# Gated DeltaNet stage: the triangular inverse without breaks beside z and v, masks first on GpSimd, convolutions in halves of their rows, the two chains at their own ticks

## The chip, the cores and the metric

The kernel runs on one core of one Trainium2 chip. The metric is the device time of one execution in microseconds (us); with several runs, their median. The engines are called by the profile's names: PE (TensorE, the matrix engine), DVE (VectorE), ACT (ScalarE), POOL (GpSimd) and SP (SyncE, which here issues the loads of the weights). SBUF is the memory on the chip, PSUM the small one that PE writes.

## The reference

Two decoder layers over 256 tokens of width 1024, in float32. Each layer is half a SwiGLU feed-forward (hidden width 2816), a token mixer, and half a feed-forward again, each behind an RMSNorm and added to the stream. Layer 1's mixer is sliding-window attention, which the change leaves alone. Layer 0's is a gated DeltaNet:

```python
proj = h @ w_in                                   # q, k, v, z: 1024 columns each; b, a: 8
qkv = silu(causal_depthwise_conv(qkv, w_conv))    # 4 taps along the tokens
q = l2norm(q) * 128 ** -0.5; k = l2norm(k)        # 8 heads of 128
beta = sigmoid(b); g = -exp(A_log) * softplus(a + dt_bias)
...
L = where(strict, (k * beta) @ k.T * decay, 0)
u, w = (I + L)^-1 [v * beta, k * beta * exp(g)]   # triangular solve per chunk and head
v_new = u - w @ S;  o = (q * exp(g)) @ S + a_qk @ v_new;  S = S * gl + k_dec.T @ v_new
...
o = rmsnorm(o, out_norm) * silu(z);  x += o @ w_out
```

What is computed is thus: projections, short convolutions, a triangular inverse per head, a recurrence over chunks of tokens, a gated norm and an output projection.

## The kernel before, in words

The kernel is one program for one core, written with a tile framework. Its scheduler fixes ahead of time in which order each engine runs its instructions; generators ("tickers") tell it in which order the pieces are offered, and `issue_after` keeps an instruction behind another. The framework's tile pools hand out a fixed number of buffers, and the first write to a tile waits until the readers of the buffer's last owner are done. Two pools matter here: psA and psB, four PSUM buffers each. Weights pass through four raw buffers and five pairs of split buffers.

A float32 product is made of three PE passes (`mm3`): each operand is split into a rounded high and a low part. Weights are split on the chip: SP loads 512 KB (`split`, L288), ACT casts the high part (L310), and DVE (L312, one instruction of 1024 columns) or POOL (L317, four of 256) takes the difference. A "chunk" is 256 columns of `w_in`, made of two such pieces (rows 0 to 511 and 512 to 1023).

The DeltaNet stage `gdn` works through chunks: z0, z1, z2, then k0 to k3, v0 to v3, q0 to q2, z3, q3. For a chunk of q, k or v, `conv` (L918) projects two tiles of 128 channels x 256 tokens, one after the other, 24 matmuls of 256 columns each into a psA buffer; ACT takes the last tap (L925), DVE the other three (L928, one instruction each, read from PSUM), and ACT's silu writes the result (L932). After each tile the ticker moves every active generator by one step.

- `gdn_gates` (L602): decay and beta from b and a, tiny DVE steps (L626 to L649), then the cumulative sums `pcum` on PE and the decay matrices `Dt`.
- `kpost` (L725): transposes k on PE (`pkn`), copies it on ACT (L729, L730), sums squares on ACT (`sumsq`, L717: four squares with an accumulator, L721), forms k k^T (`pkk`), and per chunk the factors `br` and `nbr` and two scalings of `kk2` on POOL (L747, L748).
- `blocks` (L756), for each half of the heads: cuts diagonal blocks, masks them on POOL (L768, L770) and takes a power for the norm (L772).
- `inverse` (L775): inverts the 16x16 diagonal blocks of all heads on DVE alone (L780 to L818), 24 steps, with a `yield` at two places, between which the taps of convolutions are offered.
- `chain` (L822), for each half of the heads: widens the inverse to 32, 64 and 128 with small PE matmuls (L833 `pt1`, `py`; L853; L865; L873; L881; L887), each step followed by one on ACT or DVE. Both chains are added to the ticker at the inverse's end and step together.
- `state` (L1014), `u_of` (`puu`), `pwt`, `pS`, `pws`: the recurrence over the two chunks of tokens; `o_of` (`po`, L1039), `post` (L1048: ACT square L1051, DVE sum L1052, L1054, POOL power L1055, DVE scaling L1057) and `turn` (L1062: transposes `poT`, ACT cast L1068, DVE difference L1069) end in the output projection (`acc`, `out_part`, L526).

Of the kernel before, what the change touches and what calls it, by code (L numbers as in the profile page):

```python
# [213 lines left out]
class Kern:  # L214
    def __init__(self, ctx, tc):
# [11 lines left out]
        self.early = None  # L227

# [59 lines left out]
    def split(self, src, hi, lo, shape, eng=None, cuts=1):  # L288
# [9 lines left out]
        with ExitStack() as behind:  # L298
# [14 lines left out]
            if eng is not None:  # L313

                r, h, l = (a.rearrange("p a b -> p (a b)").rearrange("p (n f) -> p n f", f=256) for a in (raw, hi, lo))
                for i in range(4):
                    eng.tensor_tensor(out=l[:, i], in0=r[:, i], in1=h[:, i].bitcast(F32), op=ALU.subtract)  # L317
# [10 lines left out]
    def wcols(self, w, c0, npool=0):  # L328
        src = w[:, c0:c0 + 256].rearrange("(k p) f -> p k f", p=P)
        pieces = [self.wpiece(src[:, 4 * i:4 * i + 4, :], 4, 256,  # L330
                              eng=self.nc.gpsimd if i >= 2 - npool else None) for i in range(2)]
        return lambda k, cs: tuple(a[:, k % 4, cs] for a in pieces[k // 4])
# [47 lines left out]
    def proj_T(self, out, w, f, nrm):  # L380
        fs = slice(f * P, (f + 1) * P)
        for k in range(KT):
            wh, wl = w(k, fs)
            self.mm3(out, wh, wl, nrm.h.hi(k), nrm.h.lo(k), k == 0, k == KT - 1)
# [296 lines left out]
    def gdn(self, nrm, prep, w_in, w_out, after):  # L681
# [9 lines left out]
        tk = Ticker()  # L691
        Dt = self.big([P, NT, H, P], "Dt")
# [32 lines left out]
        def kpost(c):  # L725
# [3 lines left out]
            nc.scalar.copy(kd[:, hs, :], pv[:, 0])  # L729
            nc.scalar.copy(keg[:, hs, :], pv[:, 1])  # L730
            sumsq(pv, ssk, 2 * c)
            yield
            beta, eG, eS = res["beta"], res["eG"], res["eS"]
# [7 lines left out]
            a = ssk[:, :, hs]  # L741
            nc.vector.tensor_scalar_add(a, a, EPS)
            nc.vector.reciprocal(br[:, :, hs], a)
            nc.vector.tensor_mul(br[:, :, hs], br[:, :, hs], beta[:, :, hs])
            nc.vector.tensor_scalar_mul(nbr[:, :, hs], br[:, :, hs], -1.0)
            yield
            nc.gpsimd.tensor_tensor(out=kd[:, hs, :], in0=kd[:, hs, :], in1=bc(eS, 0, hs), op=ALU.mult)  # L747
            nc.gpsimd.tensor_tensor(out=keg[:, hs, :], in0=keg[:, hs, :], in1=bc(eG, 1, hs), op=ALU.mult)  # L748
# [7 lines left out]
        def blocks(g):  # L756
# [4 lines left out]
            us = slice(8 * g, 8 * g + 8)  # L761
            raw = self.y1([P, 8, 32], "d32")
# [6 lines left out]
            for j, m in enumerate(("tri16", "off16")):  # L769
                nc.gpsimd.tensor_tensor(out=d2[:, j, us, :], in0=raw,  # L770
                                        in1=M[m].unsqueeze(1).to_broadcast([P, 8, 32]), op=ALU.mult)
            nc.gpsimd.tensor_tensor(out=sv[:, :, gs], in0=ssk[:, :, gs],  # L772
                                    in1=self.phalf.rearrange("p (t h) -> p t h", t=NT), op=ALU.pow)

        def inverse():  # L775
# [21 lines left out]
            yield  # L797
# [13 lines left out]
            yield  # L811
# [6 lines left out]
            nc.vector.transpose(yx[:, 1].rearrange("p u c -> p (u c)"), yx[:, 0].rearrange("p u c -> p (u c)"))  # L818
            late["yx"] = yx
            tk.add(chain(0), chain(1))  # L820

        def chain(g):  # L822
# [6 lines left out]
            def blockwise(ps, lhsT, rhs):  # L829
                for i in range(8):  # L830
                    for b in range(4):
                        bs = slice(32 * b, 32 * b + 32)
                        nc.tensor.matmul(ps[bs, i * 32:i * 32 + 32], lhsT=lhsT[bs, i, :], rhs=rhs[bs, i, :],  # L833
                                         start=True, stop=True)
# [15 lines left out]
            for i in range(8):  # L850
                for b in (0, 2):
                    e, o = slice(32 * b, 32 * b + 32), slice(32 * b + 32, 32 * b + 64)
                    nc.tensor.matmul(pt[o, i * 32:i * 32 + 32], lhsT=nf[e, i, o], rhs=X[e, i, :], start=True, stop=True)  # L853
# [8 lines left out]
            for i in range(8):  # L862
                for b in (0, 2):
                    e, o = slice(32 * b, 32 * b + 32), slice(32 * b + 32, 32 * b + 64)
                    nc.tensor.matmul(py[e, i * 32:i * 32 + 32], lhsT=t32[o, i, :], rhs=Y[o, i, :], start=True, stop=True)  # L865
# [52 lines left out]
        def conv(col0, dst, npool, start):  # L918
            w = self.wcols(w_in, col0, npool)
            for f in range(2):  # L920
                ct = col0 // P + f
                ps = self.psA("pcv")
                self.proj_T(ps[:, :T], w, f, nrm)
                c = self.c1([P, T], "cv")
                nc.scalar.activation(c, ps[:, :T], AF.Copy, scale=wc[:, 3, ct:ct + 1])  # L925
# [5 lines left out]
                with self.tc.issue_after(res["exp"].ins):  # L931
                    nc.scalar.activation(dst(f), c, AF.Silu)  # L932
                tk.tick()
            tk.add(*start, first=True)

        def zproj(c, t, w):
            pz = self.psA("pz")
            self.proj_N(pz[:, :T], w, t, nrm)
            hs = slice(2 * c, 2 * c + 2)
            nc.scalar.copy(zs[:, t, hs, :], pz[:, :T].rearrange("p (h c) -> p h c", h=2))  # L940

        def zgate(t, hs, keep=lambda ins: ins):
            z = zs[:, t, hs]
            keep(nc.scalar.activation(z, z, AF.Silu))
            keep(nc.gpsimd.tensor_tensor(
                out=z, in0=z, in1=onb.unsqueeze(1).to_broadcast([P, hs.stop - hs.start, P]), op=ALU.mult))
# [7 lines left out]
        def then(*steps):  # L954
            for st in steps:
                r = st()
                if r is not None:
                    yield from r
                    yield
# [11 lines left out]
        def zmore(n):  # L971
            for c in range(zc[0], zc[0] + n):
                w = self.wcols(w_in, 3 * D + c * 256)
                for t in range(NT):
                    zproj(c, t, w)
# [399 lines left out]
```

## Time and profile before

| what | value |
| --- | --- |
| median of 3 runs (lowest, highest) | 1019.48 us (1018.77, 1020.96) |
| the profiled execution | 1017.73 us |
| its span in the trace | 1016.0 us |
| mean granted PE clock | 0.996 |
| DeltaNet stage | from 200 to 376 us of the span, about |

The trace tells each instruction's start and length. A row of the waits names the waiting line and the one that released it, then the total, the number and the longest. The windows give each engine's busy time in a stretch, and behind them the granted PE clock, as a share of full speed. A row of groups ends with the count, the busy time, the mean of one in ns, and the idle time of the engine just ahead of them. A row of the timeline starts with the start and the length; matmuls overlap, so their pace is read from the starts.

### The profile page before, as it was taken

To read this page: it belongs to the slowest core of one execution; us is meant where nothing else is said; L and a number is where in the kernel's file an instruction comes from. 1 tells how busy PE (TensorE), PEld (TensorE's weight loads), DVE (VectorE), ACT (ScalarE), POOL (GpSimd) and SP (SyncE) were. 2 spreads that over 40 slices of the span, in tenths; PEclk is the share of its full clock that TensorE was granted. 3 is DMA by queue.
4 is the path that set the end of the run, shared out by engine and by line. 5 is a ranking of instruction groups with operands and counts; after the bars stand their busy time and mean duration, and the time that the engine had idled before them with its cause. 6 is when DMAs were issued, how large, how long until landed. Compare 5 with 4: busy or idle time off the path is not lost.

```text
span 1016.0 us, 16483 instructions
## 1 busy us (share of the span) xinstructions
PE 998.0 (98%) x6195; PEld 870.7 (86%) x6195; DVE 643.7 (63%) x975; ACT 547.8 (54%) x979; POOL 242.1 (24%) x311
## 2 busy tenths in 40 slices
PE   8999999999989999999999999999999999999997
PEld 7888888899979888888888888888898678888886
DVE  5866654666895766666546666664578756666544
ACT  5756544457856445555434655553467545555442
POOL 0125510017952301323100123320021402222100
PEclk9999999999999999999999999999999999999999
DMA  7766666644452337666666666665563426666661
GB/s 246 235 188 191 200 197 182 205 129 148 133 175 65 105 104 208 195 188 197 191 199 190 186 187 186 192 207 189 185 209 104 152 91 212 190 189 187 203 188 43
DMA packets 135316, 177.05 MB, mean 174 GB/s; under 512 B 7250, under 2 KB 120260, under 8 KB 135236
## 3 DMA queue, kind: packets, MB, share of 16 engines
q1 hardware_dynamic: 132032, 171.46, 55.3%
q10 hardware_dynamic: 3204, 4.53, 1.4%
q8 instruction: 49, 0.80, 0.3%
q14 instruction: 31, 0.25, 0.1%
HBM read 174.92 MB, written 1.05 MB: 173 GB/s over the span
## 4 chain that ended last, share of the span: by engine, by line
PE 89%; DVE 4%; ACT 3%; issue 1%; DMA 1%; POOL 1%; SPq 1%; POOLq 0%; ACTq 0%
PE pg L370 14%; PE pu L370 14%; PE acc L365 9%; PE acc L363 9%; PE acc L364 9%; PE pu L371 7%; PE pg L371 7%; PE pgu L365 2%; PE pgu L364 2%; PE pgu L363 2%; DVE wlo L312 1%; DMA raw<-in_ffn_w_gu_dram 1%; PE pcv L363 1%; PE pcv L364 1%; PE pcv L365 1%
## 5 line engine op out<-in xcount | busy, mean ns | idle before, releaser
L312 DVE TENSOR_TENSOR wlo<-raw,whi 128x1024 fp32r<-128x1024 f32 (+1 forms) x304 | 374.9, 1236 | 198.0 <-ACT whi L310 196.8
L310 ACT CAST whi<-raw 128x1024 fp32r<-128x1024 f32 (+1 forms) x318 | 330.3, 1046 | 179.5 <-PE acc L365 83.2
L370 PE MATMUL pg<-hs,whi 128*128 128x512 f32 x624 | 218.7, 392 | 0.0
L370 PE MATMUL pu<-hs,whi 128*128 128x512 f32 x624 | 218.4, 392 | 0.0
L371 PE MATMUL pu<-hs,wlo 128*128 128x256 f32 x624 | 175.4, 281 | 0.0
L371 PE MATMUL pg<-hs,wlo 128*128 128x256 f32 x624 | 174.6, 281 | 0.0
L478 POOL TENSOR_TENSOR act<-act,gate 128x256 f32<-128x256 f32 x78 | 58.6, 751 | 352.0 <-DVE act L477 337.4
L370 PEld LDWEIGHTS pg<-hs,whi 128*128 128x128 f32 x624 | 116.9, 187 | 25.3
L370 PEld LDWEIGHTS pu<-hs,whi 128*128 128x128 f32 x624 | 116.9, 187 | 25.2
L364 PE MATMUL acc<-wlo,ah 128*128 128x512 f32 (+1 forms) x340 | 128.6, 378 | 0.0
L365 PE MATMUL acc<-whi,al 128*128 128x512 f32 (+1 forms) x340 | 128.5, 378 | 0.0
L363 PE MATMUL acc<-whi,ah 128*128 128x512 f32 (+1 forms) x340 | 128.0, 378 | 0.0
L371 PEld LDWEIGHTS pg<-hs,wlo 128*128 128x128 f32 x624 | 118.2, 189 | 0.4
L371 PEld LDWEIGHTS pu<-hs,wlo 128*128 128x128 f32 x624 | 118.2, 189 | 0.0
L363 PEld LDWEIGHTS acc<-whi,ah 128*128 128x128 f32 x340 | 64.0, 188 | 12.0
L364 PEld LDWEIGHTS acc<-wlo,ah 128*128 128x128 f32 x340 | 64.0, 188 | 11.8
L365 PEld LDWEIGHTS acc<-whi,al 128*128 128x128 f32 x340 | 64.0, 188 | 11.9
L481 POOL TENSOR_SCALAR ah<-act 128x256 fp32r<-128x256 f32 x78 | 66.4, 852 | 6.7
L467 ACT COPY gate<-pg 128x256 f32<-128x256 f32 x78 | 28.7, 368 | 55.6 <-PE pg L371 55.6
L476 ACT COPY act<-pu 128x256 f32<-128x256 f32 x78 | 28.7, 368 | 54.1 <-PE pu L371 54.1
L363 PE MATMUL pcv<-hs,whi 128*128 128x256 f32 x192 | 55.1, 287 | 2.2 <-DVE cv L928 2.2
L99 POOL TENSOR_TENSOR rst<-var,mhalf 128x1 f32<-128x1 f32 x10 | 5.6, 557 | 215.6 <-DVE var L97 215.6
(340 smaller groups left out, 1576.6 us busy)
## 6 DMA issues: line engine op xcount, KB each, us to landing
raw<-in_ffn_w_gu_dram SPq DMA_DIRECT2D x156, 512.0 KB, 4.4
raw<-in_ffn_w_down_dram SPq DMA_DIRECT2D x88, 512.0 KB, 4.2
raw<-in_a_w_in_dram SPq DMA_DIRECT2D x32, 512.0 KB, 4.2
raw<-in_ffn_w_gu_dram SPq DMA_DIRECT2D x40, 256.0 KB, 4.7
raw<-in_b_w_in_dram SPq DMA_DIRECT2D x12, 512.0 KB, 4.8
raw<-in_a_w_out_dram SPq DMA_DIRECT2D x8, 512.0 KB, 3.7
raw<-in_b_w_out_dram SPq DMA_DIRECT2D x8, 512.0 KB, 3.7
nw<-in_ffn_norm_dram ACTq DMA_DIRECT2D x3, 512.0 KB, 4.0
```

Of the source, the lines that this page charges most:

```text
L99: nc.gpsimd.tensor_tensor(out=r, in0=v, in1=k.mhalf[:, 0:1], op=ALU.pow)
L310: nc.scalar.copy(hi[:, c], raw[:, c])
L312: nc.vector.tensor_tensor(out=lo[:, c], in0=raw[:, c], in1=hi[:, c].bitcast(F32), op=ALU.subtract)
L363: nc.tensor.matmul(out, lhsT=lh, rhs=rh, start=start, stop=False)
L364: nc.tensor.matmul(out, lhsT=lh, rhs=rl, start=False, stop=False)
L365: return nc.tensor.matmul(out, lhsT=ll, rhs=rh, start=False, stop=stop)
L370: nc.tensor.matmul(out, lhsT=lh, rhs=r2, start=start, stop=False)
L371: return nc.tensor.matmul(out[:, :T], lhsT=ll, rhs=rh, start=False, stop=stop)
L467: nc.scalar.copy(g, pg[:, T:])
L476: nc.scalar.copy(a, pu[:, T:])
L478: nc.gpsimd.tensor_tensor(out=a, in0=a, in1=gates[f], op=ALU.mult)
L481: ahead[2] = nc.gpsimd.tensor_scalar(oh, a, 1.0, None, op0=ALU.mult)
```

## The change

- `sumsq` squares the four transposes in place in PSUM with one ACT instruction and sums with one DVE reduce. `kpost` copies both halves of `kk2` with one ACT copy. `br` and `nbr` are made once for each half of the heads, in `blocks`, and the eight scalings of `kk2` on POOL move to `kscale`, behind v2's POOL splits.
- The power leaves `blocks`: `roots` puts the first half's behind that half's masks, the second's behind v1's splits. With `self.masks`, v1's POOL splits are put behind the second half's masks.
- `inverse` has no `yield` any more. The chains are not added at its end but after v2, each to a ticker of its own (`tkc`), and `conv` ticks the one behind each half of its first tile, the other behind its second's. The chains' matmuls are put behind the projection's last offered matmul (`late["mm"]`).
- `conv` takes both psA tiles at once and runs rows 0 to 511 of both tiles, then rows 512 to 1023 of both. The taps are a function of their own; v1's are put behind the end of the inverse.
- z3 moves from behind q2 to behind v0, in halves too, with its second piece split on POOL. POOL's share of the splits changes: the second piece of k1 and k2 (before: of k2 and k3), nothing of v0, both pieces of v1 (before: the second of each v chunk); v2 and v3 keep theirs. The gate of z on POOL is cut into pieces of 256 columns.

The diff, cut to its core:

```diff
         def sumsq(pv, ss, h0):
-            for i in range(2):
-                for t in range(NT):
-                    j = self.small([P, P], "junk", 1)
-                    nc.scalar.activation(j, pv[:, t, i, :], AF.Square, accum_out=ss[:, t, h0 + i:h0 + i + 1])
+            nc.scalar.activation(pv, pv, AF.Square)
+            nc.vector.tensor_reduce(out=ss[:, :, h0:h0 + 2], in_=pv, axis=AX.X, op=ALU.add)
...
+        def kscale():
+            eG, eS = res["eG"], res["eS"]
+            for c in range(4):
+                hs = slice(2 * c, 2 * c + 2)
+                with self.tc.issue_after(late["short"].ins):
+                    nc.gpsimd.tensor_tensor(out=kd[:, hs, :], in0=kd[:, hs, :], in1=bc(eS, 0, hs), op=ALU.mult)
+                    nc.gpsimd.tensor_tensor(out=keg[:, hs, :], in0=keg[:, hs, :], in1=bc(eG, 1, hs), op=ALU.mult)
+                yield
...
+        def roots(g, behind):
+            gs = slice(4 * g, 4 * g + 4)
+            with self.tc.issue_after(behind.ins):
+                nc.gpsimd.tensor_tensor(out=sv[:, :, gs], in0=ssk[:, :, gs],
+                                        in1=self.phalf.rearrange("p (t h) -> p t h", t=NT), op=ALU.pow)
...
                 nc.vector.tensor_add(y, y, tmp)
-            yield
             for h in (4, 8):
...
-            yield
             nc.vector.tensor_copy(t1.rearrange("p c (h r) -> p c h r", h=2),
...
-            tk.add(chain(0), chain(1))
...
             def blockwise(ps, lhsT, rhs):
-                for i in range(8):
...
+                with self.tc.issue_after(late["mm"].ins):
+                    for i in range(8):
...
-        def conv(col0, dst, npool, start):
+        def conv(col0, dst, npool, start, behind=None):
             w = self.wcols(w_in, col0, npool)
-            for f in range(2):
-                ct = col0 // P + f
-                ps = self.psA("pcv")
-                self.proj_T(ps[:, :T], w, f, nrm)
...
+            acc = [self.psA("pcv") for f in range(2)]
+            for half in range(2):
+                for f in range(2):
+                    late["mm"] = self.proj_T(acc[f][:, :T], w, f, nrm, range(4 * half, 4 * half + 4))
+                    tkc[f].tick()
+                    if half:
+                        taps(col0 // P + f, acc[f], dst(f), behind)
+                        tk.tick()
+            tk.add(*start, first=True)
+
+        def taps(ct, ps, dst, behind):
+            c = self.c1([P, T], "cv")
+            nc.scalar.activation(c, ps[:, :T], AF.Copy, scale=wc[:, 3, ct:ct + 1])
+            with ExitStack() as later:
+                if behind is not None:
+                    later.enter_context(self.tc.issue_after(behind.ins))
...
-            conv(D + c * 256, lambda f: kT[:, 2 * c + f, :], c // 2, [then(*steps)])
+            conv(D + c * 256, lambda f: kT[:, 2 * c + f, :], int(c in (1, 2)), [then(*steps)])
...
-            conv(2 * D + c * 256, lambda f: vT[:, f, :], 1, [vpost(c, vT)])
+            self.masks = late["d"] if c == 1 else None
+            conv(2 * D + c * 256, lambda f: vT[:, f, :], ((), (0, 1), (1,), (1,))[c], [vpost(c, vT)],
+                 late["inv"] if c == 1 else None)
+            if c == 0:
+                zmore(1)
+            if c == 1:
+                roots(1, self.short)
+            if c == 2:
+                late["short"] = self.short
+                for g in range(2):
+                    tkc[g].add(chain(g))
+                tk.add(kscale())
...
-            if c == 2:
-                n = 2 * zc[0]
-                w = self.wcols(w_in, 3 * D + 3 * 256)
-                for t in range(NT):
-                    zproj(3, t, w)
-                    zgate(t, slice(n, H))
-                    tk.tick()
-        tk.drain()
+        for ticker in (*tkc, tk):
+            ticker.drain()
```

The scheduler turns this into new orders. First, DVE at the end of the inverse, before. The inverse's tiles are `inv`, `tw` and `yx`; `cv` are the taps, here of q's chunks (`pcv_3323`, `pcv_3393` and `pcv_3467` are PSUM tiles of q0's second, q1's first and q1's second tile), `wlo` the splits of weights.

```order
L810 TENSOR_REDUCE inv_2793<-tw_2790 128x8x8
L928 SCALAR_TENSOR_TENSOR cv_3348<-pcv_3323,wc_1902,cv_3348 128x255
L928 SCALAR_TENSOR_TENSOR cv_3418<-pcv_3393,wc_1902,cv_3418 128x255
L812 COPY tw_2790<-inv_2793 128x512
L928 SCALAR_TENSOR_TENSOR cv_3348<-pcv_3323,wc_1902,cv_3348 128x254
L928 SCALAR_TENSOR_TENSOR cv_3418<-pcv_3393,wc_1902,cv_3418 128x254
L815 STREAM_TRANSPOSE tw_2790<-tw_2790 128x16x32
L928 SCALAR_TENSOR_TENSOR cv_3348<-pcv_3323,wc_1902,cv_3348 128x253
L312 TENSOR_TENSOR wlo_3675<-raw_3676,whi_3674 128x1024
L928 SCALAR_TENSOR_TENSOR cv_3418<-pcv_3393,wc_1902,cv_3418 128x253
L816 TENSOR_TENSOR yx_2906<-tw_2790,blk16_953 128x512
L312 TENSOR_TENSOR wlo_3795<-raw_3796,whi_3794 128x1024
```

And the same place now; `pcv_2814` and `pcv_2815` are v1's two tiles, `pcv_2893` and `pcv_2894` v2's.

```order
L313 TENSOR_TENSOR wlo_3206<-raw_3207,whi_3205 128x1024
L832 STREAM_TRANSPOSE yx_2697<-yx_2697 128x512
L957 SCALAR_TENSOR_TENSOR cv_2852<-pcv_2814,wc_1902,cv_2852 128x255
L957 SCALAR_TENSOR_TENSOR cv_2870<-pcv_2815,wc_1902,cv_2870 128x255
L957 SCALAR_TENSOR_TENSOR cv_2931<-pcv_2893,wc_1902,cv_2931 128x255
L957 SCALAR_TENSOR_TENSOR cv_2958<-pcv_2894,wc_1902,cv_2958 128x255
L957 SCALAR_TENSOR_TENSOR cv_2852<-pcv_2814,wc_1902,cv_2852 128x254
L957 SCALAR_TENSOR_TENSOR cv_2870<-pcv_2815,wc_1902,cv_2870 128x254
L957 SCALAR_TENSOR_TENSOR cv_2931<-pcv_2893,wc_1902,cv_2931 128x254
L957 SCALAR_TENSOR_TENSOR cv_2958<-pcv_2894,wc_1902,cv_2958 128x254
L313 TENSOR_TENSOR wlo_3391<-raw_3392,whi_3390 128x1024
L957 SCALAR_TENSOR_TENSOR cv_2852<-pcv_2814,wc_1902,cv_2852 128x253
```

Before, taps of q stand between the inverse's steps. Now DVE runs 25 rows, of which 23 are the inverse's, from its first step to its last, with only two splits of weights inside, then eight taps of v1 and v2, a split and the third tap of v1's first tile. The next matmul on PE behind v2 is v3's first, into `pcv_2980`, the fifth psA tile counted from `pcv_2814`.

Second, PE at the end of the stage, before: `po` are the outputs of heads (`po_3942`, `po_3958` and, one turn later, `po_4004`), `acc` the output projection, `poT` the transposes of normalized outputs.

```order
L1004 MATMUL po_3958<-u_2634,Dt_1904 128x128
L364 MATMUL acc_3979<-wlo_3899,oT_3228 128x512
L365 MATMUL acc_3979<-whi_3898,oT_3228 128x512
L363 MATMUL acc_3979<-whi_3904,oT_3228 128x512
L364 MATMUL acc_3979<-wlo_3905,oT_3228 128x512
L365 MATMUL acc_3979<-whi_3904,oT_3228 128x512
L363 MATMUL acc_3979<-whi_3910,oT_3228 128x512
L364 MATMUL acc_3979<-wlo_3911,oT_3228 128x512
L365 MATMUL acc_3979<-whi_3910,oT_3228 128x512
L1004 MATMUL po_4004<-S_3227,wq_1907 128x128
L1004 MATMUL po_4004<-u_2634,Dt_1904 128x128
L1004 MATMUL po_4004<-S_3227,wq_1907 128x128
```

Five more of `po_4004` follow there, and then `poT_4024`. Now (`po_3887`, `po_3903`, then `po_3949`, and `poT_3969`):

```order
L1049 MATMUL po_3903<-u_2592,Dt_1904 128x128
L1049 MATMUL po_3887<-u_2592,Dt_1904 128x128 x2
L1049 MATMUL po_3949<-S_3202,wq_1907 128x128
L1049 MATMUL po_3949<-u_2592,Dt_1904 128x128
L1049 MATMUL po_3949<-S_3202,wq_1907 128x128
L1049 MATMUL po_3949<-u_2592,Dt_1904 128x128
L1049 MATMUL po_3949<-S_3202,wq_1907 128x128
L1049 MATMUL po_3949<-u_2592,Dt_1904 128x128
L1049 MATMUL po_3949<-S_3202,wq_1907 128x128
L1049 MATMUL po_3949<-u_2592,Dt_1904 128x128
L1110 MATMUL poT_3969<-ident_70,on_3893 128x128 x4
L368 MATMUL acc_3923<-whi2_3864,oT_3203 128x512
```

The eight matmuls of the output projection between the two turns of `po` are gone from that place; they stand ahead of `po` now.

More of the change, by code (lines that the diff above doesn't have):

```diff
@@ L315, in split @@
                 r, h, l = (a.rearrange("p a b -> p (a b)").rearrange("p (n f) -> p n f", f=256) for a in (raw, hi, lo))
-                for i in range(4):
-                    eng.tensor_tensor(out=l[:, i], in0=r[:, i], in1=h[:, i].bitcast(F32), op=ALU.subtract)
+                with ExitStack() as masks:
+                    if self.masks is not None:
+                        masks.enter_context(self.tc.issue_after(self.masks.ins))
+                    for i in range(4):
+                        self.short = eng.tensor_tensor(out=l[:, i], in0=r[:, i], in1=h[:, i].bitcast(F32), op=ALU.subtract)
     def wpiece(self, src, a, b, eng=None, pool=None):
@@ L691, in gdn @@
         tk = Ticker()
+        tkc = [Ticker() for g in range(2)]
         Dt = self.big([P, NT, H, P], "Dt")
@@ L930, in conv @@
                         in1=c[:, s:], op0=ALU.mult, op1=ALU.add)
[L931 to L934 removed]
+            with self.tc.issue_after(res["exp"].ins):
+                nc.scalar.activation(dst, c, AF.Silu)
         def zproj(c, t, w):
```

79 lines of the change are left out of this document (43 added, 36 removed).

## The prediction

> **What bounds the kernel now.** First I read the page for the engine that sets the time.
>
> ```profile
> PE 998.0 (98%) x6195; PEld 870.7 (86%) x6195; DVE 643.7 (63%) x975; ACT 547.8 (54%) x979; POOL 242.1 (24%) x311
> ```
>
> TensorE (PE) is busy for 98% of the span. No matmul is removed or added, so the change can only win or lose time in which PE stands still or runs at a lower clock. The waits of PE in the DeltaNet stage (200 to 376 us, the only stage whose code changes), and the windows in which they fall, are next.
>
> ```profile
> PE pcv L363 <- DVE cv L928: 2.2, 2, 1.5
> PE py L833 <- ACT t L837: 2.0, 1, 2.0
> PE acc L363 <- ACT oT L1068: 0.7, 1, 0.7
> PE pt L833 <- DVE yx L818: 0.5, 1, 0.5
> PE pt L853 <- DVE X L844: 0.5, 1, 0.5
> ```
>
> ```profile
> 280.00:290.00 10.00, 8.50 (x71) 8.33 (x71) 10.00 (x21) 5.95 (x10) 4.60 (x5) 1.00 0.62 182
> 290.00:300.00 10.00, 8.34 (x184) 7.68 (x183) 10.00 (x14) 4.61 (x8) 7.43 (x8) 1.00 0.42 141
> 300.00:310.00 10.00, 8.03 (x224) 7.69 (x225) 8.23 (x20) 6.33 (x18) 2.35 (x3) 0.83 0.34 111
> ```
>
> The columns behind the window's length are PE, weight loads, DVE, ACT, POOL (busy us and count), then the granted clock. From 280 to 300 DVE is busy without a gap and PE waits for it; from 300 to 310 the clock is 0.83, which costs 1.7 us more. The rows of waits add up to 5.9 us. A wait costs somewhat more than its row says:
>
> ```profile
> 283.05 0.28 PE L364 MATMUL pcv<-hs,whi 128*128 128x256 f32 x1
> 283.17 0.28 PE L365 MATMUL pcv<-hs,wlo 128*128 128x256 f32 x1
> 284.95 0.36 PE L363 MATMUL pcv<-hs,whi 128*128 128x256 f32 x1 [1.50 <-DVE cv L928]
> ```
>
> A matmul of 256 columns starts 0.12 us after the one before it; here 1.78 us pass, so the wait of 1.50 costs 1.66. With 0.16 for each of six waits, **before loses 5.9 + 1.0 + 1.7 = 8.6 us** in this stage. That is all that the change can win.
>
> **The convolutions' first part (k).** The gates' pcum stands after 67 projection matmuls of k in PE's order now, after 99 before: 32 x 0.12 = 3.8 us earlier. It needs gg from DVE.
>
> ```profile
> 222.60 0.17 DVE L642 TENSOR_SCALAR gr<-gr 128x16 f32<-128x16 f32 x1
> 222.81 0.63 DVE L641 TENSOR_TENSOR gr<-gr,gs 128x16 f32<-128x16 f32 x1
> 227.58 0.17 DVE L647 SCALAR_TENSOR_TENSOR gg<-gr,expA 128x16 f32<-128x16 f32 x1
> 222.68 2.83 POOL L317 TENSOR_TENSOR wlo<-raw,whi 128x256 fp32r<-128x256 f32 x4 [23.38 <-ACT whi L310]
> 228.99 0.29 PE L652 MATMUL pcum<-gg,sufftri 128*128 128x16 f32 x2
> ```
>
> gg ends at 227.75, 1.24 us before PE's use, so 3.8 - 1.2 = 2.6 us would be missing. DVE is rid of one split of 1.22 us ahead of it, since POOL takes k's second chunk now: 1.4 at row prices, and I take 1.0 (0 to 2.2), as four of the tiny operations ran into POOL's split (0.63 instead of 0.17) and may not do so where the order differs. The squares of k leave ACT's four pairs for one pass and a DVE reduce. That shortens ACT, but the PSUM tile of the transposes is now given back by DVE, in order behind its taps. Nearest below is nothing, above the 1.5 us of the longest wait for a tap; I take 0.8, of which the waits of two later transposes are made. POOL's half of v1, v2 and z can come late (POOL does 12 such splits in a row): 0.4 to 1.2, I take 0.8.
>
> **The inverse in one go.** This is the term that decides. All of its steps, eight taps and three weight splits now follow each other on DVE (the order under the change shows them), and v3's first matmul waits for the ninth tap, because psA has four buffers: v3's first tile takes the one of v1's first half, whose three taps are put behind the inverse. So between the end of v0 and v3 PE has z's 48 matmuls, 96 of v1 and v2 and four transposes, and no more.
>
> ```profile
> 298.87 0.66 PE L714 MATMUL pvn<-ident,vT 128*128 128x128 f32 x4
> 270.00:298.00 28.00, 8.80 (x17) 1.00 0.55 172
> 270.00:298.00 28.00, 1.75 (x4) 1.00 0.55 172
> L784 DVE COPY inv<-inv 128x256 f32<-128x256 f32 x1 | 0.8, 826 | 0.0
> L818 DVE STREAM_TRANSPOSE yx<-yx 128x512 f32<-128x512 f32 x1 | 0.7, 695 | 0.0
> 280.21 1.22 DVE L312 TENSOR_TENSOR wlo<-raw,whi 128x1024 fp32r<-128x1024 f32 x1
> 297.50 1.60 DVE L928 SCALAR_TENSOR_TENSOR cv<-pcv,wc,cv 128x255 f32<-128x255 f32 x4
> L925 ACT ACTIVATE cv<-pcv,wc 128x256 f32<-128x256 f32 x24 | 11.2, 472 | 4.3 <-PE pcv L365 4.3
> ```
>
> The two rows of 28 us are DVE's busy time with the inverse's tiles tw and itmp. PE's cover is 144 x 0.12 + 4 x 0.13 = 17.8 us, and 0.8 more with POOL's late pieces: 18.6. DVE's chain from the end of v0: ACT's copy 0.5, three taps of 0.40, a tiny step 0.3, a split 1.2, together 3.2; the inverse 8.8 + 1.75 + 0.83 + 0.70 = 12.1; two splits inside it 2.4; eight taps 3.2; another split 1.2; the ninth tap 0.4. Sum 22.5, so **PE would wait 3.9 us** even if nothing is late. Two things make it later. The mask from POOL hangs on the last sum of squares, on four tiny steps and on two POOL operations:
>
> ```profile
> L768 POOL TENSOR_TENSOR d<-d,knbr 128x256 f32<-128x256 f32 x2 | 1.2, 618 | 0.0
> L770 POOL TENSOR_TENSOR d<-d,tri 128x256 f32<-128x256 f32 x2 | 1.5, 740 | 0.1
> ```
>
> Copy, square and reduce of 0.6 to 0.7 each from 1.4 us ahead of v0's end, tiny steps of 0.65, 0.62 and 0.74 end about 3.9 us after it, 0.7 behind DVE's own 3.2. And POOL works beside the whole inverse: 8 splits of v1, a power, 4 of v2, 8 scalings, 4 of v3, some 19 us. A neighbour of that kind shows in the trace:
>
> ```profile
> 273.04 1.75 DVE L312 TENSOR_TENSOR wlo<-raw,whi 128x1024 fp32r<-128x1024 f32 x1
> 272.09 6.84 POOL L317 TENSOR_TENSOR wlo<-raw,whi 128x256 fp32r<-128x256 f32 x8
> ```
>
> DVE's split took 1.75 instead of 1.22 while POOL split. About half of the inverse already ran beside POOL in before, so I add 0.5 for each of three splits and for two steps that did not: 2.5 (0 to 5). The wait ahead of v3 is then 3.9 + 0.7 + 2.5 = 7.1 us (2 to 11). The Trainium skill, page "SBUF — State Buffer", section "Who interferes with whom", says that a DVE instruction with two SBUF inputs and a GpSimd instruction lock each other out for a whole instruction. The tiny steps above (0.17 alone, 0.63 beside POOL) agree; by the rule alone each such step of the inverse would wait out a POOL operation of 0.7, which is the third rival.
>
> After the 2.0 us wait for t the clock fell to half for 3.4 us (the 0.83 of that window), so I put the same 1.7 us (0 to 3.4) behind the longer wait.
>
> **The chains later.** Spread over q, each chain step has conv matmuls between it and the next, which hide ACT's and DVE's 1 to 2 us. The waits for yx, t and X go; I count nothing in their place. But state(), u for the second half and po come later too, behind the last q conv, with less work around them. In before they had this:
>
> ```profile
> 344.69 1.27 ACT L1051 ACTIVATE on<-po 128x512 f32<-128x512 f32 x2 [2.97 <-PE po L1004]
> 345.32 1.36 DVE L1052 TENSOR_REDUCE so<-on 128x4 f32<-128x512 f32 x2 [1.67 <-ACT on L1051]
> 346.59 0.28 DVE L1054 TENSOR_TENSOR fo<-ssq,so 128x4 f32<-128x4 f32 x2
> 346.82 1.98 POOL L1055 TENSOR_TENSOR fo<-fo,mhalf 128x4 f32<-128x4 f32 x2 [5.53 <-DVE fo L1054]
> 347.86 2.16 DVE L1057 SCALAR_TENSOR_TENSOR on<-po,fo,zs 128x128 f32<-128x128 f32 x8 [0.99 <-POOL fo L1055]
> 347.01 0.38 PE L1004 MATMUL po<-S,wq 128*128 128x128 f32 x2
> 348.79 1.62 PE L1065 MATMUL poT<-ident,on 128*128 128x128 f32 x8
> 350.42 1.08 ACT L1068 CAST oT<-poT 128x512 fp32r<-128x512 f32 x2
> 351.06 0.50 PE L363 MATMUL acc<-whi,oT 128*128 128x512 f32 x1 [0.65 <-ACT oT L1068]
> ```
>
> From the square at 344.69 to the first normalized head (347.86 + 0.27) are 3.4 us. Before, PE had eight matmuls of the output projection and the next po there, up to 348.79. Now the projection's matmuls stand ahead of po, and only the next po (347.01 to 348.79: 1.8 us) is between: a wait of 1.6. The transposes then wait for the cast as before (0.65 with 0.16), and po itself, close behind pws, may wait 0.3 for u. Together 2.7 (0.8 to 4).
>
> **Sum.** After: 1.0 + 0.8 + 0.8 + 7.1 + 1.7 + 2.7 = 14.1 us lost, before 8.6: 5.5 us more. The profiled execution took 1017.73 (span 1016.0 and 1.7 around it) and would become 1023.2; the median of the three runs, 1019.48, lies 1.75 above it, and on that scale the forecast is **1025.0**. A measurement of this kernel tells about 0.2% (2 us) from no change.
>
> **Rivals.** *The wait ahead of v3 stays short* (faster). The inverse's rows overlap: one step starts some 0.08 before its predecessor's row ends,
>
> ```profile
> 292.92 0.85 DVE L816 TENSOR_TENSOR yx<-tw,blk 128x512 f32<-128x512 f32 x1
> 293.69 2.87 DVE L312 TENSOR_TENSOR wlo<-raw,whi 128x1024 fp32r<-128x1024 f32 x1
> ```
>
> and with 24 steps the inverse is 10.2 instead of 12.1. Without lateness and contention the wait is 2.0, and a wait of 1.5 in before was not followed by a lower clock. Losses 0.3 + 0.4 + 0.8 + 2.0 + 0 + 2.0 = 5.5: 3.1 us less than before, 1016.4. It decides if PE waits for less than about 3 us there. Against it speaks that POOL is occupied during the whole inverse. Chance 0.22, for all times over 0.2% faster.
>
> *The losses trade places* (no difference): a wait of about 3.5, half of the clock's loss, 0.9 and a tail of 2 give 0.6 + 0.8 + 0.8 + 3.5 + 0.9 + 2.0 = 8.6, or 1019.5. That the rearrangement does nothing belongs here, but the order shows it on every engine. Chance 0.20.
>
> *DVE and POOL take turns* (slower still): 10 two-input steps of the inverse that ran alone before, and three splits, wait 0.7 each, which is 9 instead of 2.5. The wait is 13.6 and the time 1031.5. The tiny steps speak for it, the split at 273.04 (plus 0.53, not plus 2.8 for four POOL pieces) against. Chance 0.13.
>
> The forecast itself, a wait of 4 to 10 us, has 0.45. Slower is 0.45 + 0.13 = 0.58. The range leaves out a tenth on each side: the lower half of the faster case, below 1015.5, and the upper part of the turn-taking one, above 1032.
>
> **What would show it.** In the profile after: a wait of v3's first pcv for a tap of v1 as PE's longest, some 7 us; the waits for t, yx and X gone; a window with a clock under 1 right behind it; DVE busy without gap from the mask to that tap, its rows longer than before; a wait at poT of 1 to 2 us. A v3 wait under 3 us, or none because taps are released sooner, would make the forecast wrong; so would a new wait at pcum or at the pkn transposes beyond 2 us.

## The result and the profile after

The changed kernel takes 1029.41 us (median of 5 runs, 1026.54 to 1031.62) against 1019.48 before: a ratio of 1.0092, 95% interval 1.0069 to 1.0115, so 9.4 us (7.0 to 11.7) slower; the two medians lie 9.9 us apart. The forecast was 1025.0 with a range of 1015.5 to 1032.0. The profiled execution after took 1030.19 us with a span of 1028.4 and a granted clock of 0.99.

Where PE waits in the DeltaNet stage now (the same view as in the prediction):

```profile
PE pcv L368 <- DVE cv L957: 9.4, 1, 9.4
PE poT L1110 <- DVE on L1102: 1.8, 1, 1.8
PE pcv L370 <- POOL wlo L321: 1.2, 2, 0.7
PE acc L368 <- ACT oT L1113: 0.7, 1, 0.7
PE pcum L658 <- DVE gg L653: 0.4, 1, 0.4
```

The waits for the chain's t, for yx and for X are gone, as is the wait for q's taps. One wait stands in their place, and it is larger than all the old ones together. The windows around it and around the end of the stage:

```profile
270.00:280.00 10.00, 6.33 (x48) 5.69 (x47) 9.83 (x17) 4.62 (x7) 10.00 (x11) 1.00 0.62 193
280.00:290.00 10.00, 3.10 (x14) 3.13 (x15) 7.92 (x15) 2.63 (x5) 10.00 (x12) 0.53 0.39 126
...
360.00:370.00 10.00, 9.42 (x34) 7.62 (x35) 5.32 (x13) 2.09 (x5) 1.45 (x1) 0.71 0.18 52
```

The columns behind the window's length are PE, weight loads, DVE, ACT and POOL, then the granted clock. PE is empty for most of 277 to 287 while DVE and POOL are full. The clock is down in two stretches, where before had one (0.83): the 0.53 here, which runs on into the next window (0.96), and the 0.71, which begins in the window ahead of it (0.95).

Most of the time was lost inside the stage. In the timeline, the first and the last landmark of the stage before,

```profile
202.40 0.34 PE L363 MATMUL pab<-hs,wabh 128*64 128x256 f32 x1 [0.24 <-ACT hs L115]
368.90 0.39 PE L363 MATMUL pgu<-whi,hs 128*128 128x512 f32 x1
```

and after:

```profile
203.78 0.33 PE L368 MATMUL pab<-hs,wabh 128*64 128x256 f32 x1 [0.24 <-ACT hs L115]
381.38 0.39 PE L368 MATMUL pgu<-whi,hs 128*128 128x512 f32 x1
```

From the gates' first matmul to the feed-forward's first, the stage took 166.5 us before and 177.6 after, 11.1 more; 1.4 us of the profiled difference lie ahead of the stage, in code that is the same. "Stage" below means this length, which is free of where an execution starts.

The wait of 9.4 us can be read off DVE's timeline:

```profile
261.63 1.21 DVE L313 TENSOR_TENSOR wlo<-raw,whi 128x1024 fp32r<-128x1024 f32 x1
264.17 1.08 DVE L796 STREAM_TRANSPOSE tw<-d 128x512 f32<-128x512 f32 x1 [1.32 <-POOL d L780]
...
272.48 1.71 DVE L313 TENSOR_TENSOR wlo<-raw,whi 128x1024 fp32r<-128x1024 f32 x1
...
279.88 1.63 DVE L313 TENSOR_TENSOR wlo<-raw,whi 128x1024 fp32r<-128x1024 f32 x1
281.44 0.70 DVE L832 STREAM_TRANSPOSE yx<-yx 128x512 f32<-128x512 f32 x1
282.07 3.16 DVE L957 SCALAR_TENSOR_TENSOR cv<-pcv,wc,cv 128x255 f32<-128x255 f32 x8
285.15 1.21 DVE L313 TENSOR_TENSOR wlo<-raw,whi 128x1024 fp32r<-128x1024 f32 x1
286.29 1.63 DVE L957 SCALAR_TENSOR_TENSOR cv<-pcv,wc,cv 128x253 f32<-128x253 f32 x4
```

POOL's masks ahead of it:

```profile
261.77 1.55 POOL L778 TENSOR_TENSOR d<-d,knbr 128x256 f32<-128x256 f32 x1 [5.77 <-DVE cv L957]
263.40 0.74 POOL L780 TENSOR_TENSOR d<-d,tri 128x256 f32<-128x256 f32 x1
```

and PE, from z3's first matmul to v3's first:

```profile
257.87 0.28 PE L368 MATMUL pz<-whi,hs 128*128 128x256 f32 x1
...
277.00 0.50 PE L370 MATMUL pcv<-hs,wlo 128*128 128x256 f32 x2 [0.48 <-POOL wlo L321]
286.90 0.55 PE L368 MATMUL pcv<-hs,whi 128*128 128x256 f32 x1 [9.40 <-DVE cv L957]
```

The inverse starts at 264.17, as soon as the mask is there, and ends at 282.1. Eight taps, a split and the ninth tap follow, and PE resumes 0.1 us after that tap ends (286.29 + 0.48 of one tap). It is the queue that the prediction drew up, row for row; its start came later than forecast.

### The profile page after: what moved, and what is told of

Its sections match the earlier page's. It is cut to its first block, busy times and chain, and to the rows that moved or that the text cites. A ratio compares the mean times of both kernels' runs of the same rounds, so it can differ in the third digit from the quotient of the medians.

```text
span 1028.4 us, 16430 instructions
## 1 busy us (share of the span) xinstructions
PE 1004.1 (98%) x6195; PEld 873.7 (85%) x6195; DVE 651.2 (63%) x974; ACT 543.8 (53%) x917; POOL 248.5 (24%) x319
## 4 chain that ended last, share of the span: by engine, by line
PE 88%; DVE 5%; ACT 2%; issue 2%; DMA 1%; POOL 1%; POOLq 0%; SPq 0%; ACTq 0%; DVEq 0%
PE pg L375 14%; PE pu L375 14%; PE acc L368 9%; PE acc L370 9%; PE acc L369 9%; PE pu L376 7%; PE pg L376 7%; PE pgu L370 2%; PE pgu L369 2%; PE pgu L368 2%; PE pcv L368 1%; DVE wlo L313 1%; PE pcv L370 1%; PE pcv L369 1%; DVE cv L957 1%
## 5 line engine op out<-in xcount | busy, mean ns | idle before, releaser
L368 PEld LDWEIGHTS acc<-whi,ah 128*128 128x128 f32 x340 | 64.0, 188 | 12.1
L321 POOL TENSOR_TENSOR wlo<-raw,whi 128x256 fp32r<-128x256 f32 x60 | 49.6, 858 | 43.5 <-ACT whi L311 43.5
```

The costliest lines, as they stand in the source:

```text
L321: self.short = eng.tensor_tensor(out=l[:, i], in0=r[:, i], in1=h[:, i].bitcast(F32), op=ALU.subtract)
L368: nc.tensor.matmul(out, lhsT=lh, rhs=rh, start=start, stop=False)
```

## The experiments

All ratios are to the kernel before, run in turn with them on the same chip; the changed kernel's own is 1.0092. In the diffs, lines of the changed kernel or of the kernel before stand with a minus.

**Is it the queue on DVE ahead of the ninth tap?** First, v1's taps are not put behind the inverse:

```diff
-                 late["inv"] if c == 1 else None)
+                 None)
```

> The changed kernel with v1's taps no longer put behind the inverse's end. Theory A (the wait ahead of v3 is the queue on DVE in front of the tap that frees the PSUM tile): in the order four taps, one split and one transpose leave that queue, 1.6 + 1.2 + 0.6 us, so the wait falls from 9.4 to about 6.0 us and the time by 3 to 4 us. Theory B (the inverse is stretched by POOL's work beside it, whatever stands behind it): the wait stays at 8.5 to 9.4, the time within 1 us of the changed kernel.

```profile
PE pcv L368 <- DVE cv L957: 5.5, 1, 5.5
```

The wait fell from 9.4 to 5.5 us and the ratio to 1.0051 (1.0034 to 1.0069), that is by 4.2 us; theory A said 6.0 and 3 to 4. The stages of the two profiled executions, which both have the second stretch of low clock, differ by 3.2 us (177.6 and 174.4). So a third to nearly half of the loss against before hangs on that one line. Next, v1 is also ready earlier, since POOL splits only its second piece:

```diff
-                 late["inv"] if c == 1 else None)
+                 None)
-            conv(2 * D + c * 256, lambda f: vT[:, f, :], ((), (0, 1), (1,), (1,))[c], [vpost(c, vT)],
+            conv(2 * D + c * 256, lambda f: vT[:, f, :], ((), (1,), (1,), (1,))[c], [vpost(c, vT)],
```

> The changed kernel with v1's taps free and only the second piece of v1 split on POOL instead of both. v1 is then done earlier on PE and its three taps stand between steps of the inverse. Theory A: the queue in front of the ninth tap loses 5 to 6 us, the wait falls to 3 to 4.5 us and the time by 5 to 7. Theory B: POOL has four operations of 24 fewer beside the inverse, so the wait falls by 1 us at most.

```profile
PE py L848 <- issue: 3.0, 1, 3.0
PE pcv L368 <- DVE cv L957: 2.7, 1, 2.7
```

The wait for the tap fell to 2.7, somewhat under theory A's 3 to 4.5, but the ratio stayed at 1.0085 (1.0070 to 1.0101), where 5 to 7 us of gain had been expected. A wait of 3.0 us with no releaser ("issue") came up between the chains' small matmuls, and the clock was at half for 3.4 us behind the wait for the tap and for 6.8 us from the end of the other. The theory of the queue holds; the sum that was made with it did not, for a reason that is taken up below under "issue".

**How much of it is POOL's work beside the inverse?** POOL writes zeros instead of subtracting for v1, v2 and v3. This leaves out the low part of those weights:

```diff
-                        self.short = eng.tensor_tensor(out=l[:, i], in0=r[:, i], in1=h[:, i].bitcast(F32), op=ALU.subtract)
+                        self.short = (eng.memset(l[:, i].bitcast(F32), 0.0) if self.nolow else
+                                      eng.tensor_tensor(out=l[:, i], in0=r[:, i], in1=h[:, i].bitcast(F32), op=ALU.subtract))
...
+            self.nolow = c > 0
...
+        self.nolow = False
```

> The changed kernel in which POOL fills its low parts of v1, v2 and v3 with zeros instead of subtracting (the low part of these weights is left out), so that POOL is nearly idle beside the inverse; the order stays. What POOL's neighbourhood costs: theory A, the queue alone is 3.9 us too long and POOL adds the rest: the inverse's first to last row shrinks from 18.0 us by 3 to 4, the wait ahead of v3 from 9.4 to about 6. Theory B (taking turns with POOL is nearly all of it): it shrinks by 6 or more and the wait is under 3.5.

```profile
262.30 1.10 DVE L798 STREAM_TRANSPOSE tw<-d 128x512 f32<-128x512 f32 x1 [1.33 <-POOL d L782]
...
266.41 0.17 DVE L814 TENSOR_TENSOR inv<-inv,itmp 128x8 f32<-128x8 f32 x1
...
277.14 0.69 DVE L834 STREAM_TRANSPOSE yx<-yx 128x512 f32<-128x512 f32 x1
```

From the first to the last row the inverse takes 15.5 us, with one tap (0.4) inside; in the changed kernel it is 282.1 - 264.2 = 17.9. Both have two splits inside. POOL's subtractions thus cost DVE 2.8 us there, a little under theory A's 3 to 4 and far from theory B's 6. POOL was not nearly idle, as the expectation has it: its zeros, the power, the scalings and a last split of another chunk fill it from 262.9 to 278.1 without a gap. So 2.8 is the share of the subtractions, and the least for POOL as a whole. The smallest steps show it best: 0.17 here, though POOL was at work with its power and its zeros, and 0.67 beside the subtractions of the changed kernel.

```profile
267.22 0.67 DVE L812 TENSOR_TENSOR inv<-inv,itmp 128x8 f32<-128x8 f32 x1
```

The wait itself is still 8.0 us and not 6, because PE, which no longer waits for POOL's pieces, also comes to v3 earlier: from z3's first matmul to v2's last it has 17.9 us of work (256.01 to 273.86) instead of 19.6. The ratio, 1.0082 (1.0049 to 1.0116), can't be told from the changed kernel's. The queue is too long without these subtractions too; without any work of POOL it was not tried.

**Is an inverse without breaks harmful by itself?** The kernel before with only the two `yield` lines of `inverse` taken out:

```diff
                 nc.vector.tensor_add(y, y, tmp)
-            yield
             for h in (4, 8):
...
-            yield
             nc.vector.tensor_copy(t1.rearrange("p c (h r) -> p c h r", h=2),
```

> The kernel before with nothing changed but the two breaks of the inverse taken out. Theory A: the scheduler still puts the taps of q between the steps, since they are ready; within 2 us of before. Rival (an inverse without breaks holds DVE by itself): a wait of PE for a tap of 5 us or more, and 4 us or more slower than before.

```profile
PE pcv L363 <- DVE cv L926: 2.9, 2, 1.7
PE py L831 <- ACT t L835: 1.7, 2, 1.5
```

The ratio is 0.9993 (0.9980 to 1.0006). Taps that are ready still go between the steps. It is not the missing breaks that hurt. In the changed kernel v1's taps were kept behind the inverse's end, and the run with them free shows what that cost.

**Do the late chains make the end of the stage slow?** Both chains are stepped at each half of a tile:

```diff
-                    tkc[f].tick()
+                    for g in range(2):
+                        tkc[g].tick()
```

> The changed kernel with both chains stepped at every half of a tile, twice as often. Theory A: the wait ahead of v3 stays at 9.4, since it lies ahead of the chains; the end of the stage (waits of 1.8 for the normalized heads and 0.7 for the cast, and the second stretch at half clock) was due to the late chains and goes, 3 to 5 us less. Rival: the end of the stage is set by q3, not by the chains; then nothing changes there, within 1 us.

```profile
PE pcv L368 <- DVE cv L958: 9.4, 1, 9.4
PE poT L1111 <- DVE on L1103: 1.8, 1, 1.8
PE py L848 <- issue: 1.6, 1, 1.6
...
PE acc L368 <- ACT oT L1114: 0.7, 1, 0.7
```

The waits at poT and for oT stayed to a tenth, so theory A's part on the end of the stage fell (the half clock behind them is absent from this profiled execution; the last section comes back to that). The ratio went up to 1.0151 (1.0131 to 1.0172): the "issue" wait is here too, with 3.4 us at half clock behind it, as soon as the first steps of both chains stand together. They cost some 3.5 us (1.6 with 0.16, and half of 3.4) of the 6.0 above the changed kernel; the rest is not explained.

**Does z3 cover the end?** The changed kernel with z3 between q2 and q3 again:

```diff
-            if c == 0:
-                zmore(1)
...
+            if c == 2:
+                n = 2 * zc[0]
+                zmore(1)
+                for t in range(NT):
+                    zgate(t, slice(n, H))
```

> The changed kernel with z3 back between q2 and q3. Theory A: z3's 5.8 us no longer cover the inverse, so PE's waits up to v3 grow by 4 to 6 us, while z3 at the end covers the chain from state to po: the waits of 1.8 and 0.7 there and the half clock behind them (5 us in all) mostly go. Within 2.5 us of the changed kernel. Rival: the end of the stage has nothing to do with z3; then the waits there stay and the kernel is 4 us slower than the changed one.

```profile
PE pcv L368 <- DVE cv L957: 6.6, 1, 6.6
PE pcv L370 <- POOL wlo L321: 2.1, 4, 0.9
PE poT L1108 <- DVE on L1100: 1.8, 1, 1.8
PE pvn L721 <- ACT vT L961: 1.8, 2, 1.2
```

The rows of waits up to v3 add up to 10.9 us (6.6 + 2.1 + 1.8 and 0.4), against 10.6 in the changed kernel (9.4 + 1.2): they did not grow by the 4 to 6 us of theory A, but there are eight waits now instead of three. From the gates' first matmul, v3 starts after 80.1 us here and after 83.1 in the changed kernel, which has z3's 5.8 us done by then, so 2.8 us were lost up to v3, only part of which the rows show. The wait of 1.8 at the end stayed. The ratio is 1.0128 (1.0100 to 1.0156), 3.7 us above the changed kernel's: the rival. So neither the chains' pace nor z3's place sets the wait at poT. In the orders of all these kernels the projection's matmuls stand ahead of the last po; which part of the change put them there was not tried.

**The mirror image:** the kernel before with only z3 moved, behind v0:

```diff
             conv(2 * D + c * 256, lambda f: vT[:, f, :], 1, [vpost(c, vT)])
+            if c == 0:
+                zmore(1)
...
-            if c == 2:
-                n = 2 * zc[0]
-                w = self.wcols(w_in, 3 * D + 3 * 256)
-                for t in range(NT):
-                    zproj(3, t, w)
-                    zgate(t, slice(n, H))
-                    tk.tick()
```

> The kernel before with only z3 moved, from behind q2 to behind v0. Theory A: z3 gives DVE 5.8 us more beside the inverse, so PE's waits for taps (2.2 us) and for yx and X (1.0) go; at the end of the stage state, u and po lose z3's cover, and waits of 1 to 3 us and a stretch at half clock can come instead. 3 us faster (without them) to 2 us slower (with them). Rival (z3's place changes nothing, since DVE's queue moves along with PE): within 1 us, with the same waits as before.

The ratio was 0.9982 (0.9963 to 1.0001), and in more rounds:

> The kernel before with only z3 moved behind v0, once more and in more rounds, since its first interval just touched no change. If the first result holds: 0.1 to 0.3% faster. If it was chance: an interval around no change.

0.9995 (0.9987 to 1.0004). No change that can be told. The waits moved instead of going:

```profile
PE pcv L363 <- DVE cv L928: 2.7, 2, 1.9
PE py L833 <- ACT t L837: 1.7, 2, 1.1
```

The waits for yx and X did go, those for taps are as large as ever: DVE's queue moves along with PE, which was the rival.

**The cheap part:** the kernel before with only the squares' sums changed.

```diff
-            for i in range(2):
-                for t in range(NT):
-                    j = self.small([P, P], "junk", 1)
-                    nc.scalar.activation(j, pv[:, t, i, :], AF.Square, accum_out=ss[:, t, h0 + i:h0 + i + 1])
+            nc.scalar.activation(pv, pv, AF.Square)
+            nc.vector.tensor_reduce(out=ss[:, :, h0:h0 + 2], in_=pv, axis=AX.X, op=ALU.add)
```

> The kernel before with only the squares' sums changed (one square on ACT in place, one reduce on DVE). Theory A: ACT was not what PE waits for and DVE gets 0.7 us eight times outside the stretch from 260 to 300; within 1.5 us of before. Rival: the four reduces for k delay taps and the PSUM tiles of the transposes; 2 to 3 us slower.

0.9990 (0.9977 to 1.0002): 1.0 us, within theory A's bounds. This part neither made nor cost time that can be told.

**Versions that might beat both.** z3 early together with the squares' sums (the last two diffs):

> The kernel before with z3 behind v0 and the squares' sums changed as in the change. Theory A (two small gains at different places): 0.2 to 0.4% faster. Rival: they remove the same stretch at half clock, so no more than z3 alone.

1.0023 (1.0014 to 1.0032), slower, by a wait that neither part has alone:

```profile
PE py L831 <- issue: 2.6, 1, 2.6
```

And z3 early with its second piece split on POOL:

```diff
-                w = self.wcols(w_in, 3 * D + c * 256)
+                w = self.wcols(w_in, 3 * D + c * 256, int(c == 3))
```

> The kernel before with z3 behind v0 and z3's second piece split on POOL. Theory A: DVE, which PE waits for in this stretch, loses 1.2 us, so 0.5 to 1.5 us faster than z3 moved alone. Rival: POOL is full from 257 to 272, the masks come later by the 2.8 us of four splits and with them the inverse and the chains; 1 to 3 us slower than z3 moved alone.

0.9978 (0.9962 to 0.9995), the only version that beats the kernel before, by some 2 us as the ratio has it and by 1.0 us as the medians have it (1016.80 and 1017.81); its ratio is 1.7 parts in a thousand lower than z3 moved alone in the same rounds, though the two intervals overlap. DVE's two waits for taps became one:

```profile
PE pcv L363 <- DVE cv L928: 1.9, 1, 1.9
```

**What is the "issue" wait?** The changed kernel has none, and makes the first step of each chain at a place of its own. Each chain makes its first 64 matmuls twice:

```diff
-            nc.scalar.copy(t32, blockwise(self.psB("pt1"), off, X0))
+            first = self.psB("pt1")
+            blockwise(first, off, X0)
+            nc.scalar.copy(t32, blockwise(first, off, X0))
```

> The changed kernel in which each chain makes its first 64 small matmuls twice. 128 more matmuls of some 11 ns each are 1.3 us. Theory A (PE runs out of supplied instructions when some 180 small matmuls follow each other closely, as where both chains stepped together): a new wait of 1 to 3 us with no releaser (issue) inside the small matmuls, and perhaps half clock behind it. Rival (those waits were for ACT or DVE): no such wait, 1.3 us slower at most.

The small matmuls in PE's timeline of that run (the convolution's are left out):

```profile
289.83 1.29 PE L848 MATMUL pt<-yx,d 32*32 32x32 f32 x128
...
292.54 0.89 PE L848 MATMUL pt<-yx,d 32*32 32x32 f32 x81
295.61 0.86 PE L848 MATMUL pt<-yx,d 32*32 32x32 f32 x47 [2.18 <-issue]
```

The wait came, 2.2 us, in the middle of a step whose operands had been there since its first matmul; half clock for 6.8 us stands behind it. The ratio is 1.0158 (1.0136 to 1.0180), 6.7 us above the changed kernel's for 1.3 us of work. In the run with v1 early it looks the same, without matmuls of the convolution between the two chains' steps:

```profile
287.04 1.31 PE L848 MATMUL pt<-yx,d 32*32 32x32 f32 x128
288.26 0.64 PE L848 MATMUL py<-yx,t 32*32 32x32 f32 x50
291.92 0.43 PE L848 MATMUL py<-yx,t 32*32 32x32 f32 x14 [3.02 <-issue]
```

In all four runs with such a wait of over 1 us (v1 early, chains denser, z3 with the squares' sums, and this one) PE had run 178 to 209 of the small matmuls in close order. That PE runs out of supplied instructions is theory A's reading, and the traces bear it out. Here are the windows from the start of the span into the wait, for v1 early, for this run and for the chains denser:

```profile
0.00:290.00 290.00, 282.67 (x1872) 251.87 (x1872) 197.16 (x305) 167.35 (x278) 93.89 (x133) 0.99 0.60 185
...
0.00:294.50 294.50, 278.75 (x1872) 247.00 (x1872) 195.27 (x297) 165.19 (x273) 94.32 (x136) 0.98 0.59 181
...
0.00:294.50 294.50, 279.46 (x1872) 248.03 (x1872) 195.85 (x300) 164.86 (x274) 93.96 (x135) 0.98 0.59 181
```

PE stands at three different places of the program, but each time after the same 1872 matmuls and 1872 weight loads. With z3 back it stands 0.5 us after the same number, though there the small matmuls come 64 at a time; with z3 and the squares' sums it stands 126 matmuls further on (1998). The trace also has a queue of transfers that it calls instruction, with 49 packets of 16 KB in the changed kernel and 50 in this run, which differs by 128 matmuls and their weight loads:

```profile
q8 instruction: 49, 0.80, 0.3%
...
q8 instruction: 50, 0.82, 0.3%
```

That is one packet for some 253 of the 12390 matmuls and weight loads. In all five runs PE goes on 1.25 to 1.47 us after such a packet has ended (in this run it lasts from 293.26 to 294.24, and PE goes on at 295.61). So PE stood for its instructions, by all that the traces show. The density of the small matmuls decides whether it has to: an estimate from these numbers is that 128 of them use up a packet in 1.3 us, while a packet takes 1.0 us and the 1.25 to 1.47 behind it. The changed kernel comes to the same matmul at 297.3, 1.4 us after its packet's end (295.90), and so just in time. Why the packets do not come sooner stays open. The Trainium skill, page "Runtime: NRT & Kernel Launch", section "Instruction fetch mechanics", says that the sequencer refills its instruction memory in blocks of 16 KiB by a DMA queue of its own, and that this is mostly hidden. The trace agrees on the blocks; in these runs the refill was not hidden, at 0.5 to 3.0 us.

## Why the prediction was right, point by point

The direction, the place and the mechanism were right, and the measured time lies inside the range; the forecast of 5.5 us was 3.9 too small. Part of the total is luck: the term for k was 1.4 too high and hid as much of what the other terms had too low.

- **Before loses 8.6 us, and all of it can be won.** The old waits but the last one (0.7 for oT) are gone, as forecast.
- **The wait ahead of v3:** 7.1 forecast, 9.4 measured. PE's work between v0 and v3, from 257.87 to the end of v2's last row at 277.50, is 19.6 instead of 18.6, in part because its two waits for POOL's pieces came to 1.2 and not 0.8. The inverse starts 6.3 behind v0's end instead of 3.9. That is the term that was mis-sized, and it was so on paper already: the times that the prediction lists for the way to the mask come to 2.4 to 2.7, not to 3.9. In the trace the last sum of squares ends 1.7 behind v0's end (at 259.53; listed 0.4 to 0.7), the tiny steps take 1.2 with a tap among them (listed 0.65), POOL's first mask operation starts another 1.0 later, when DVE's taps are done, and takes 1.55 instead of 0.62, beside DVE's split of 261.63. The inverse with its two splits: 17.9 instead of 12.1 + 2.4 + 2.5 = 17.0. Taps and split: 4.7 instead of 4.8. Together 6.3 + 17.9 + 4.7 - 19.6 = 9.3, and 0.1 until PE starts.
- **POOL beside the inverse:** 2.5 forecast. Against the rows of before it is 17.9 - 12.1 - 2.4 = 3.4, and the run with POOL light gives 2.8 for the subtractions alone. The rival that DVE and POOL take turns for whole operations (9) did not come true over the inverse as a whole, though its smallest steps do show it (0.67 instead of 0.17). The Trainium skill's rule on two SBUF inputs ("SBUF — State Buffer", "Who interferes with whom") is for a GpSimd instruction that reads SBUF, not for one that only writes it. The trace bears out that such steps are held up by the subtractions and not by the zeros (0.17 at 266.61 and 266.81 with POOL light, beside the zeros of 266.58); a price of 0.7 for every one of them is too high here.
- **Half clock behind it:** 1.7 forecast. By the windows the stretch lasted from about 280.5 to 290.8, and from PE's return at 286.9 half of 3.9 us is 1.9.
- **The end of the stage:** 2.7 forecast for its waits. The wait at poT was 1.8 (1.6 forecast), that for the cast 0.7, and po did not wait for u:

```profile
358.75 1.16 PE L1110 MATMUL poT<-ident,on 128*128 128x128 f32 x4 [1.84 <-DVE on L1102]
360.58 0.79 PE L368 MATMUL acc<-whi,oT 128*128 128x512 f32 x1 [0.68 <-ACT oT L1113]
```

  What the sum lacked is a second stretch at half clock, from about 359.1 to 365.9, the 0.71 of its window: with PE back at 360.6 it cost some 2.6 us. The wait at poT was counted from the projection's matmuls standing ahead of po, and that held. The other reason given, that state and po come late because the chains do, fell with the two runs that moved chains and z3.
- **k's part:** 1.0 + 0.8 forecast; 0.4 at pcum, and no wait at the transposes. POOL's pieces: 0.8 forecast, 1.2 measured.
- **The sum with what was measured:** 9.4 + 1.9 + 2.5 + 2.6 + 0.4 + 1.2 = 18.0 and 0.16 for each of six waits, 19.0, against 8.6: 10.4 of the stage's 11.1 us.

The faster rival needed a wait under 3 us ahead of v3. The run with v1 early had 2.7 and was slower than before all the same, by 8.5 parts in a thousand. That rival counted no half clock and no wait among the chains' steps, and would have been wrong even where its condition was met.

## What to carry to other kernels

Work that is held behind a long step also holds the buffers that it would have freed; count how much the waiting engine has left until it needs the oldest of them, and compare that with the whole queue in front of the release, splits and taps included. A wait that is removed is not yet time won: where the engine then runs into a burst of small instructions or into a lower clock, it can pay as much again at the next place. Test parts of a change alone as well as in pairs, since two that cost nothing apart (z3 early, the sums of squares) cost 2 us together.

## What the runs showed of the hardware that was not expected

PE can stand for its own instructions. Waits with no releaser, of 1.6 to 3.0 us, appeared where 178 to 209 matmuls of 32x32 followed each other within a few microseconds, and one of 0.5 us where they came 64 at a time. All of them ended 1.25 to 1.47 us after a 16 KB packet of the instruction queue, and in four runs they stood after the same 1872 matmuls. The kernel before runs 128 and again 128 with 2.0 us between, without one; its packet (299.92 to 300.88) came while PE waited for t.

The clock's stretches at half speed lasted 3.4, 6.8 or 10.2 us. Waits of 9.4 and 8.0 us came with 10.2, one of 5.5 with 6.8, but so did the "issue" waits of 2.2 and 3.0, and two waits of 0.6 and 1.1 close together came with 3.4 (z3 early, in more rounds; the clock is 0.72 from 300 to 306). Yet the run with only the squares' sums changed waited 2.5 us for t, and its clock was 1.00 from 290 to 320. At the end of the stage the waits of 1.8 and 0.7 us were followed by half clock in the profiled executions of the changed kernel and of the runs with the taps free, with v1 early, with POOL light and with the first matmuls twice, but not in those with the chains denser and with z3 back, whose waits there were the same. So the length of a wait alone does not decide it. The stretch may come and go between executions of one kernel: those of the changed kernel have a granted clock of 0.990 or 0.991 (1029.41 to 1031.62 us) or of 0.994 (1026.54 and 1027.52 us), and 6.8 us at half clock are 3.4 us, or 0.003 of the clock. Only the profiled execution has a trace, so this is not shown.
